# RWKV, HGRN and a weight stream on one TensorE: an order written by hand in place of the planner's

## Chip, cores and metric

One core of one Trainium2 chip runs the whole program. The metric is the device time of one execution in microseconds, the median of several runs. The engines are TensorE (PE, with its weight loads as PEld), VectorE (DVE), ScalarE (ACT), GpSimd (POOL) and SyncE (SP), which here only issues DMAs.

## The reference

One layer of a streaming encoder on 256 tokens of width 1024, float32. Three mixers run side by side on one combined projection of the normalised input, and a mixture of experts follows:

```
h = LN(x)
feats = h @ w_in          # SSD | RWKV-7 | HGRN2 | 3 gates
y_a = SSD(feats_a); y_b = RWKV7(feats_b); y_c = HGRN2(feats_c)
m = sum_i sigmoid(gate_i) * (y_i @ w_br_i)
h = LN(alpha*h + m @ w_out)
h = LN(alpha*h + MoE(h))  # 16 experts, top 1 group, top 2
```

RWKV is a recurrence over tokens (a delta rule: decay, rank-one correction, new key and value). HGRN is a gated linear recurrence. The kernel computes both in four chunks of 64 tokens: inside a chunk with matrices, from chunk to chunk with a state.

## The kernel before

**Weight streams.** Nearly all matrix work with weights from memory goes through `stream` (L331). SP loads four 128-row blocks of a 256-column slice (512 KB) into a `raw` buffer (L339, a ring of four). `split` (L180) makes two parts of each pair of blocks, `whi` by an ACT copy (L183) and `wlo` by a DVE subtraction (L184), each 128x512 and in a ring of four. Then PE makes six matmuls of 256 columns for each block, in a PSUM tile `st` of a ring of three: L366 to L368, or L358 to L360 where the tokens are the stationary side. Such six matmuls are called a pass here; `feat` (L371), one slice of 256 columns, is eight passes. Splits carry a priority far ahead of all else.

**The second half of the mixers** (`mixers`, L726) starts when the RWKV's preparations are done. In program order it holds these parts:

- `rwkv_solve` (L566): a triangular solve for a batch of two head pairs, 32 steps on DVE (L593, L595). Its operands come from DRAM, and its answer goes there (L599) and comes back in another layout (L605).
- `rwkv_solve_off` (L609): two DVE transposes of that answer (L618), 32 small matmuls (L623), two ACT copies, 32 more (L631) and two copies.
- `rwkv_b` (L637): the chain over four chunks, for two head pairs side by side. Each chunk has three steps: `w` (L654, and L658 from the state, then an ACT copy, L660), `u` (L662, ACT copies L663 and L665), and the state update (L670, then DVE at L674 or L676). Behind the chunks stand the outputs (L687, L691), their mean and variance, and the group norm (L694 to L708). `rwkv_out` (L710) transposes and finishes a pair (L715, L717, L722 to L724).
- `hgrn` (L838): three `feat` slices (q, v and gate), gates and exponentials on DVE, POOL and ACT, then four groups of PE work with ACT and DVE between them: L879 and L885, L893, L905 and L909, L920.
- `gates` (L780): eight more `feat` slices whose only successor is a tanh.

`rwkv_b`, `rwkv_out` and `hgrn` run four times (head pairs 0 and 1, 2 and 3, and so on), and `rwkv_solve_off` before the first and the third. The SSD mixer follows (`ssd_prep`, L989, with convolutions at L928 and L931), then the branches, the output projection and the experts.

**What sets the order.** The code is emitted in program order. A planner replays it against a timeline of its own and gives each engine its instructions in an order of priority and readiness; an instruction that is ready may so overtake others. On the chip each engine takes its queue in that order. `high_priority` moves a block ahead, `issue_after` holds one back. In the expert stage, `manual_schedule` already orders PE by hand: within its block the instructions of PE are issued as emitted.

The functions that the diff touches:

Of the kernel before, what the change touches and what calls it, by code (L numbers as in the profile page):

```python
# [7 lines left out]
F32 = mybir.dt.float32  # L8
# [5 lines left out]
OP = mybir.AluOpType  # L14
# [59 lines left out]
DNP = 60  # L74

# [64 lines left out]
class Kern:  # L140
# [190 lines left out]
    def stream(self, w, c0, ncol, xhi, xlo, ps, tokens):  # L331
# [5 lines left out]
        for kh in range(KT // KH):  # L337
# [11 lines left out]
            with self.tc.high_priority(offset=MMP):  # L349
                for kk in range(KH):  # L350
# [10 lines left out]
                    else:  # L361
                        for f in range(nf):
# [6 lines left out]
                                             stop=sp and f == nf - 1)  # L369

    def feat(self, c0, tokens=False, ncol=256, other=False):  # L371
        ps = self.pz.tile([128, 2, 256], F32, name="z") if other else self.pst.tile([128, 2, 256], F32, name="st")
        self.stream(self.A["w_in"], c0, ncol, self.hhi, self.hlo, ps, tokens)
        return ps
# [234 lines left out]
    def rwkv_solve_off(self, st):  # L609
# [23 lines left out]
        for h in range(2):  # L633
            q = slice(h * 64, h * 64 + 32)
            nc.scalar.activation(tt[q, :, 32:64], yps[q], AF.Copy)

    def rwkv_b(self, i0, st):  # L637
# [7 lines left out]
        zs = [self.zs[f] for f in range(2)]  # L645
        for c in range(4):
            for f in range(2):
                q = st["pairs"][i0 + f]
                sc, bkt, uv, ars, pe = (q[n] for n in ("sc", "bkt", "uv", "ars", "pe"))
                ch = banks[f][:, 0:192].rearrange("p (j n) -> p j n", j=3)  # L650
                z = zs[f]
# [11 lines left out]
                nc.scalar.activation(uv[hs[0], c, 0, :], ch[hs[0], 1, :], AF.Copy)  # L663
                if U1:
                    nc.scalar.activation(uv[hs[1], c, 1, :], ch[hs[1], 1, :], AF.Copy)  # L665
                else:
                    nc.vector.tensor_copy(uv[hs[1], c, 1, :], ch[hs[1], 1, :])
                if c < 3:
                    for h in range(2):
                        nc.tensor.matmul(ch[hs[h], 2, :], bkt[:, c, hs[h]], uv[:, c, h, :], start=True, stop=True,  # L670
                                         tile_position=(0, 64 * h))
                    for h in hs:
                        if c == 0:
                            nc.vector.tensor_copy(z[h, 0, h], ch[h, 2, :])  # L674
                        else:
                            nc.vector.scalar_tensor_tensor(z[h, c, h], z[h, c - 1, h], pe[h, c - 1:c], ch[h, 2, :],  # L676
                                                           op0=OP.mult, op1=OP.add)
# [30 lines left out]
        nc.vector.tensor_tensor(yc, yc, r[:, :, None].to_broadcast([128, 8, 64]), op=OP.mult)  # L708

# [16 lines left out]
    def mixers(self):  # L726
# [53 lines left out]
    def gates(self, ms):  # L780
        nc = self.nc
        for m in ms:
            ps = self.feat(COL_GATE + m * 256)
            nc.scalar.activation(self.gt[:, 2 * m:2 * m + 2, :], ps, AF.Tanh, scale=0.5)  # L784

# [51 lines left out]

    def hgrn(self, j):  # L838
# [4 lines left out]
        ps = self.feat(COL_Q + j * 256)  # L843
        q = a.new([128, 2, L], "q", 2)
# [899 lines left out]
```

## Time and profile before

| | us |
|---|---|
| median of 3 runs | 812.57 (811.85 to 814.41) |
| the profiled execution | 813.39 |
| its span, first to last instruction | 811.6 |
| PE busy | 777.7 (96%) |
| PE weight loads busy | 598.9 (74%) |
| DVE busy | 513.1 (63%) |
| ACT busy | 369.0 (45%) |
| mean granted clock of PE | 0.983 of full |

Matmuls are pipelined and their ends are modelled: in a view of the timeline, two matmuls that start 0.12 us apart each show 0.28 us. So the time that PE needs is read from start to start, and a PE that is busy in the table may still be off its best pace. The page divides the span into 40 slices, of 20.3 us each, and its digits are tenths. The second half of the mixers runs from about 168 to 424 us, the experts from about 575.

### The profile page before, as it was taken

What the parts mean: (1) busy time and instruction counts of PE and PEld (TensorE: products, weight loads), DVE (VectorE), ACT (ScalarE), POOL (GpSimd) and SP (SyncE); (2) the same over time, 40 slices, a digit from 0 to 9 for tenths busy, and PEclk for the clock granted to TensorE, in tenths of its full rate; (3) what the DMA queues carried; (4) which work ended last, traced back from release to release, by engine and by line L of the source; (5) the groups of instructions that cost most, each with busy time, mean ns of one, the idle gap of its engine ahead of it and who ended that gap; (6) DMA issues with size and microseconds to landing.
All of it is one profiled execution on the core that took longest, in us unless ns stands there. A gap on an engine that the chain in (4) does not pass through costs nothing. (4 is left out here: it accounts for less than half of the span.)

```text
span 811.6 us, 16395 instructions
## 1 busy us (share of the span) xinstructions
PE 777.7 (96%) x6306; PEld 598.9 (74%) x6306; DVE 513.1 (63%) x1166; ACT 369.0 (45%) x817; POOL 137.7 (17%) x211
## 2 busy tenths in 40 slices
PE   7999999999999999999998999999999999999991
PEld 5898899988997998998797999999444434443440
DVE  6897899999987555576589897785612211221146
ACT  4765555575446555645486764452512121211111
POOL 3364633631002002010012111000000000001201
PEclk9999999999999999999899999999999999999995
DMA  7544555493463463565188579995999999999961
GB/s 236 173 126 117 115 144 138 137 215 103 131 151 111 130 182 107 147 195 178 45 270 305 163 221 277 328 313 177 368 386 387 387 386 386 387 388 385 387 229 55
DMA packets 146493, 183.92 MB, mean 227 GB/s; under 512 B 25561, under 2 KB 94440, under 8 KB 146408
## 3 DMA queue, kind: packets, MB, share of 16 engines
q1 hardware_dynamic: 142888, 176.91, 66.5%
q0 software_dynamic: 1472, 3.21, 1.6%
q10 hardware_dynamic: 2048, 2.70, 1.1%
q8 instruction: 51, 0.84, 0.4%
q14 instruction: 34, 0.28, 0.1%
HBM read 180.13 MB, written 2.65 MB: 225 GB/s over the span
## 5 line engine op out<-in xcount | busy, mean ns | idle before, releaser
L184 DVE TENSOR_TENSOR wlo<-raw,whi 128x512 fp32r<-128x512 f32 x268 | 190.2, 720 | 75.2 <-ACT whi L183 64.1
L183 ACT ACTIVATE whi<-raw 128x512 fp32r<-128x512 f32 x268 | 165.0, 623 | 152.7 <-PE st L367 117.3
L366 PE MATMUL st<-hhi,whi 128*128 128x256 f32 (+1 forms) x744 | 209.6, 289 | 2.4 <-ACT arena L784 1.4
L368 PE MATMUL st<-hhi,wlo 128*128 128x256 f32 (+1 forms) x744 | 210.5, 292 | 0.8 <-DVE wlo L184 0.8
L367 PE MATMUL st<-hlo,whi 128*128 128x256 f32 (+1 forms) x744 | 207.8, 287 | 0.0
L368 PEld LDWEIGHTS st<-hhi,wlo 128*128 128x128 f32 (+1 forms) x744 | 139.4, 191 | 8.5 <-issue 3.9
L366 PEld LDWEIGHTS st<-hhi,whi 128*128 128x128 f32 (+1 forms) x744 | 140.0, 191 | 7.3 <-issue 2.4
L367 PEld LDWEIGHTS st<-hlo,whi 128*128 128x128 f32 (+1 forms) x744 | 139.7, 191 | 2.7 <-issue 1.4
L1455 PE MATMUL b<-arena,xg 128*64 128x512 f32 x288 | 78.8, 596 | 0.0
L367 PE MATMUL st<-ylo,whi 128*128 128x256 f32 x192 | 52.5, 284 | 1.9 <-DVE ylo L184 1.9
L366 PE MATMUL st<-yhi,whi 128*128 128x256 f32 x192 | 53.0, 284 | 0.3 <-ACT whi L183 0.2
L368 PE MATMUL st<-yhi,wlo 128*128 128x256 f32 x192 | 52.1, 283 | 0.0
L1455 PEld LDWEIGHTS b<-arena,xg 128*64 128x64 f32 x288 | 23.8, 137 | 38.0 <-issue 34.5
L1528 DVE SCALAR_TENSOR_TENSOR elo<-b,egs,ehi 128x512 fp32r<-128x512 f32 x15 | 11.2, 750 | 60.7 <-ACT ehi L1527 60.7
L1508 PE MATMUL b<-arena,ehT 128*64 128x512 f32 x144 | 43.0, 596 | 0.0
L367 PEld LDWEIGHTS st<-ylo,whi 128*128 128x128 f32 x192 | 35.5, 189 | 2.6 <-DVE ylo L184 2.3
L1497 ACT ACTIVATE ehT<-b 128x256 f32<-128x256 f32 x16 | 6.2, 390 | 68.1 <-PE b L1496 68.1
L366 PEld LDWEIGHTS st<-yhi,whi 128*128 128x128 f32 x192 | 35.7, 189 | 0.8 <-ACT whi L183 0.4
L1489 DVE SCALAR_TENSOR_TENSOR ehi<-ehi,b 128x256 f32<-128x256 f32 x16 | 6.0, 418 | 47.0 <-PE b L1455 47.0
L368 PEld LDWEIGHTS st<-yhi,wlo 128*128 128x128 f32 x192 | 35.4, 189 | 0.2 <-issue 0.2
L593 DVE TENSOR_TENSOR arena<-arena 128x1 f32<-128x1 f32 (+15 forms) x64 | 33.1, 517 | 1.0
L1370 POOL TENSOR_TENSOR arena<-arena 128x512 f32<-128x512 bf16 x4 | 4.5, 1156 | 171.6 <-PE b L1455 171.6
(453 smaller groups left out, 1432.2 us busy)
## 6 DMA issues: line engine op xcount, KB each, us to landing
raw<-in_w_in_dram SPq DMA_DIRECT2D x102, 512.0 KB, 3.7
arena<-in_exp_w_gate_dram SPq DMA_DIRECT2D x40, 512.0 KB, 10.7
arena<-in_exp_w_down_dram SPq DMA_DIRECT2D x34, 512.0 KB, 10.8
arena<-in_exp_w_up_dram SPq DMA_DIRECT2D x32, 512.0 KB, 10.8
xsl<-in_exp_w_up_dram SPq DMA_DIRECT2D x32, 512.0 KB, 10.8
xsl<-in_exp_w_down_dram SPq DMA_DIRECT2D x20, 512.0 KB, 10.8
xsr<-in_exp_w_gate_dram SPq DMA_DIRECT2D x16, 512.0 KB, 10.7
raw<-in_w_br_rwkv_dram SPq DMA_DIRECT2D x8, 512.0 KB, 4.2
```

What stands on the lines that cost most here:

```text
L183: nc.scalar.activation(hi, raw, AF.Copy)
L184: nc.vector.tensor_tensor(lo, raw, hi.bitcast(F32), op=OP.subtract)
L366: nc.tensor.matmul(o, hi[:, kq, fs], xhi[:, k, :], start=st and f == 0, stop=False)
L367: nc.tensor.matmul(o, hi[:, kq, fs], xlo[:, k, :], start=False, stop=False)
L368: nc.tensor.matmul(o, lo[:, kq, fs], xhi[:, k, :], start=False, stop=sp and f == nf - 1)
L593: nc.vector.tensor_tensor(po, tu[:, :n, :t + 1], eu[:, :t + 1, t][:, None, :].to_broadcast([128, n, t + 1]), op=OP.mult)
L1370: nc.gpsimd.tensor_tensor(o, x[1], x[2], op=OP.add)
L1455: nc.tensor.matmul(ps[hs[e]], xg[:, k, hs[e]], W[nm, e, k // 2][:, k % 2, :], start=k == 0, stop=k == KT - 1)
L1489: nc.vector.scalar_tensor_tensor(th[:, c], th[:, c], 0.5, q["pu"][:, c], op0=OP.mult, op1=OP.mult)
L1497: nc.scalar.activation(q["hT"][:, 2 * j:2 * j + 2], tp, AF.Copy)
L1508: nc.tensor.matmul(pd[hs[e], :], q["hT"][:, k, hs[e]], W["exp_w_down", e, (n, k // 2)][:, k % 2, :], start=k == 0, stop=k == 3)
L1528: nc.vector.scalar_tensor_tensor(lo, pd, q["gs"], hi.bitcast(F32), op0=OP.mult, op1=OP.subtract)
```

## The change

Four functions become generators that yield between their steps: `stream` (as `streaming`, one yield for each pass), `rwkv_solve_off` (two), `rwkv_b` (one for each step of a chunk) and `hgrn` (four). The three slices of `hgrn` become a generator of their own, `hgrn_in`; `rwkv_out` and one slice of `gates` get generators around them. In `rwkv_b` the two head pairs' parts of a step now stand together, where one pair's three steps stood ahead of the other's; nothing is computed otherwise. `interleave` runs them in turns inside a `manual_schedule` block for PE alone. A turn emits one step of the RWKV chain, one of the HGRN chain (a yield of n lets a chain rest for n turns) and FILL = 2 passes of the streams: `hgrn_in` in order, each as soon as the HGRN pair two before it is done, otherwise a gate slice, once the first RWKV pair is done. Passes that are left over come behind the chains. The second solve is emitted ahead of the first `rwkv_solve_off` instead of behind it.

```diff
-    def stream(self, w, c0, ncol, xhi, xlo, ps, tokens):
+    def stream(self, *a):
+        for _ in self.streaming(*a):
+            pass
+
+    def streaming(self, w, c0, ncol, xhi, xlo, ps, tokens):
...
+                    yield
...
+    def feating(self, c0, tokens=False):
+        ps = self.pst.tile([128, 2, 256], F32, name="st")
+        yield from self.streaming(self.A["w_in"], c0, 256, self.hhi, self.hlo, ps, tokens)
         return ps
...
         for c in range(4):
+            ws = []
             for f in range(2):
-                q = st["pairs"][i0 + f]
-                sc, bkt, uv, ars, pe = (q[n] for n in ("sc", "bkt", "uv", "ars", "pe"))
-                ch = banks[f][:, 0:192].rearrange("p (j n) -> p j n", j=3)
-                z = zs[f]
+                (sc, bkt, uv, ars, pe), ch, z = P[f], chs[f], zs[f]
...
+                ws.append(w)
+            yield 1
+            for f in range(2):
+                (sc, bkt, uv, ars, pe), ch, w = P[f], chs[f], ws[f]
                 for h in hs:
                     nc.tensor.matmul(ch[h, 1, :], tt[h, (i0 + f) * 4 + c, :], w[h], start=True, stop=True)
+                for h in range(2):
+                    nc.scalar.activation(uv[hs[h], c, h, :], ch[hs[h], 1, :], AF.Copy)
+            yield 1
+            if c == 3:
+                break
+            for f in range(2):
+                (sc, bkt, uv, ars, pe), ch, z = P[f], chs[f], zs[f]
+                for h in range(2):
+                    nc.tensor.matmul(ch[hs[h], 2, :], bkt[:, c, hs[h]], uv[:, c, h, :], start=True, stop=True,
+                                     tile_position=(0, 64 * h))
+                for h in hs:
...
+            yield 1
...
+    def rwkv_outs(self, i0, st):
+        for i in (i0, i0 + 1):
+            yield 1
+            self.rwkv_out(i, st)
...
         self.ssd_dt()
-        MARK('rwS')
-        self.rwkv_solve_off(s0)
-        MARK('rwS1')
         with self.tc.high_priority(offset=PSV):
             self.rwkv_solve(1, s1)
-        for j in range(4):
-            if j == 2:
-                MARK('rwS')
-                self.rwkv_solve_off(s1)
-            MARK('rwB%d' % j)
-            self.rwkv_b(2 * (j % 2), (s0, s1)[j // 2])
-            for i in (0, 1):
-                self.rwkv_out(2 * (j % 2) + i, (s0, s1)[j // 2])
-            MARK('hgrn%d' % j)
-            self.hgrn(j)
-        MARK('gates')
-        self.gates(range(NG - NZ - NY))
+        self.interleave(s0, s1)
...
+    def interleave(self, s0, s1):
+
+        self.hgin, done = [], dict(rw=0, hg=0)
+
+        def rwkv():
+            yield from self.rwkv_solve_off(s0)
+            for j in range(4):
+                st = (s0, s1)[j // 2]
+                if j == 2:
+                    yield from self.rwkv_solve_off(s1)
+                yield from self.rwkv_b(2 * (j % 2), st)
+                yield 4
+                yield from self.rwkv_outs(2 * (j % 2), st)
+                done["rw"] += 1
+                yield 1
+
+        def hgrn():
+            for j in range(4):
+                while len(self.hgin) <= j:
+                    yield 1
+                yield from self.hgrn(j)
+                done["hg"] += 1
+                yield 1
+
+
+        tiles = [(self.hgrn_in(j), lambda j=j: done["hg"] > j - 2) for j in range(4)]
+        gates = [(self.gating(m), lambda m=m: done["rw"] > 0) for m in range(NG - NZ - NY)]
+        queue, now = [tiles, gates], []
+
+        def fill():
+
+            while True:
+                if not now:
+                    for q in queue:
+                        if q and q[0][1]():
+                            now.append(q.pop(0)[0])
+                            break
+                    else:
+                        return False
+                try:
+                    next(now[0])
+                    return True
+                except StopIteration:
+                    now.clear()
+
+        chains = [[rwkv(), 0], [hgrn(), 0]]
+        with self.tc.manual_schedule(engines={mybir.EngineType.PE}):
+            while chains:
+                for c in list(chains):
+                    c[1] -= 1
+                    if c[1] <= 0:
+                        try:
+                            c[1] = next(c[0])
+                        except StopIteration:
+                            chains.remove(c)
+                for _ in range(FILL):
+                    fill()
+            while fill():
+                pass
...
+    def hgrn_in(self, j):
+
+        nc, a = self.nc, self.hga
+        ps = yield from self.feating(COL_Q + j * 256)
...
+        self.hgin.append((q, v, tg))
+
+    def hgrn(self, j):
+
+        nc = self.nc
+        a, mp = self.hga, self.pmm
+        hs = [slice(0, 64), slice(64, 128)]
+        q, v, tg = self.hgin[j]
...
```

## Rows read from the trace of the kernel before

**Rows 1.** Page, 40 slices: PE's busy time and granted clock in tenths

```profile
PE   7999999999999999999998999999999999999991
PEclk9999999999999999999899999999999999999995
```

**Rows 2.** Stretches: length, busy PE, PEld, DVE, ACT, POOL; clock, DMA, GB/s

```profile
220.00:240.00 20.00, 20.00 (x201) 18.99 (x200) 19.71 (x47) 9.87 (x21) 0.96 (x1) 1.00 0.55 144
...
380.00:400.00 20.00, 18.05 (x164) 13.77 (x163) 11.58 (x33) 8.58 (x32) 0.00 (x0) 0.83 0.18 54
```

**Rows 3.** PE's timeline, 387 to 400: start, duration, engine, line, [idle before, releaser]

```profile
387.70 0.34 PE L654 MATMUL ch<-arena 128*64 128x64 f32 x4
387.96 0.33 PE L658 MATMUL ch<-arena 64*64 64x64 f32 x4
...
390.46 0.81 PE L670 MATMUL ch<-arena 128*64 128x64 f32 x8 [0.43 <-ACT arena L665]
...
394.90 0.58 PE L366 MATMUL st<-hhi,whi 128*128 128x256 f32 x1
...
399.36 0.34 PE L654 MATMUL ch<-arena 128*64 128x64 f32 x4
```

**Rows 4.** PE's timeline, 222 to 226: a run of stream matmuls between two steps

```profile
222.44 0.39 PE L359 MATMUL st<-wlo,hhi 128*128 128x256 f32 x1
222.66 0.28 PE L367 MATMUL st<-hlo,whi 128*128 128x256 f32 x1
...
224.69 0.28 PE L360 MATMUL st<-whi,hlo 128*128 128x256 f32 x1
224.90 0.45 PE L662 MATMUL ch<-arena 64*64 64x64 f32 x8
225.27 0.39 PE L358 MATMUL st<-whi,hhi 128*128 128x256 f32 x1
```

**Rows 5.** PE's timeline, the two longest of its short waits

```profile
244.55 0.39 PE L359 MATMUL st<-wlo,hhi 128*128 128x256 f32 x1 [0.79 <-DVE wlo L184]
...
366.52 0.39 PE L366 MATMUL st<-hhi,whi 128*128 128x256 f32 x1 [1.09 <-ACT arena L784]
```

**Rows 6.** PE's timeline, 160 to 178

```profile
168.04 0.37 PE L358 MATMUL st<-whi,hhi 128*128 128x256 f32 x1
...
176.42 0.24 PE L623 MATMUL mm<-arena 32*32 32x32 f32 x2
```

**Rows 7.** SP's queue, 160 to 175: DMA issues

```profile
165.16 2.47 SPq L599 DMA_DIRECT2D td<-arena  x4
...
169.47 2.87 SPq L605 DMA_DIRECT2D arena<-td  x4
```

**Rows 8.** DVE's timeline, 175 to 176

```profile
175.91 0.70 DVE L618 STREAM_TRANSPOSE arena<-arena 32x512 f32<-32x512 f32 x1
```

**Rows 9.** All engines' timeline, 390 to 394: DVE and ACT of the chain

```profile
390.97 1.17 DVE L676 SCALAR_TENSOR_TENSOR arena<-arena,pe,ch 64x64 f32<-64x64 f32 x4
...
393.19 0.22 ACT L660 ACTIVATE arena<-ch 128x64 f32<-128x64 f32 x1 [0.68 <-PE ch L658]
```

**Rows 10.** DVE's groups of 168 to 235: count, busy us, mean ns, idle before

```profile
L593 DVE TENSOR_TENSOR arena<-arena 128x1 f32<-128x1 f32 (+31 forms) x32 | 16.6, 519 | 0.6
L595 DVE TENSOR_REDUCE arena<-arena 128x1 f32<-128x1 f32 (+31 forms) x32 | 10.9, 341 | 0.6
```

**Rows 11.** DVE's timeline, 290 to 302: the group norm of the second pair

```profile
292.74 0.42 DVE L694 TENSOR_REDUCE gmean<-ch 128x4 f32<-128x256 f32 x1 [0.48 <-PE ch L691]
...
301.17 0.68 DVE L708 TENSOR_TENSOR arena<-arena,gr_y 128x512 f32<-128x512 f32 x1
```

**Rows 12.** PE's groups of 168 to 427

```profile
L366 PE MATMUL st<-hhi,whi 128*128 128x256 f32 x400 | 112.9, 291 | 1.4 <-ACT arena L784 1.4
...
L358 PE MATMUL st<-whi,hhi 128*128 128x256 f32 x64 | 18.7, 292 | 0.0
```

**Rows 13.** Page, groups of the whole span: the streams' subtraction

```profile
L184 DVE TENSOR_TENSOR wlo<-raw,whi 128x512 fp32r<-128x512 f32 x268 | 190.2, 720 | 75.2 <-ACT whi L183 64.1
```

More of the change, by code (lines that the diff above doesn't have):

```diff
@@ L74 @@
 DNP = 60
+FILL = 2
 PARAMS = [("ln_in_g", 8), ("ln_in_b", 8), ("rwkv_mu", 26), ("rwkv_w0", 8), ("rwkv_a0", 8), ("rwkv_k_k", 8),
@@ L373, in feat @@
         self.stream(self.A["w_in"], c0, ncol, self.hhi, self.hlo, ps, tokens)
+        return ps
+    def feating(self, c0, tokens=False):
+        ps = self.pst.tile([128, 2, 256], F32, name="st")
+        yield from self.streaming(self.A["w_in"], c0, 256, self.hhi, self.hlo, ps, tokens)
         return ps
@@ L645, in rwkv_b @@
         zs = [self.zs[f] for f in range(2)]
+        P = [[st["pairs"][i0 + f][n] for n in ("sc", "bkt", "uv", "ars", "pe")] for f in range(2)]
+        chs = [banks[f][:, 0:192].rearrange("p (j n) -> p j n", j=3) for f in range(2)]
         for c in range(4):
+            ws = []
             for f in range(2):
-                q = st["pairs"][i0 + f]
-                sc, bkt, uv, ars, pe = (q[n] for n in ("sc", "bkt", "uv", "ars", "pe"))
-                ch = banks[f][:, 0:192].rearrange("p (j n) -> p j n", j=3)
-                z = zs[f]
+                (sc, bkt, uv, ars, pe), ch, z = P[f], chs[f], zs[f]
                 for h in range(2):
@@ L660, in rwkv_b @@
                 nc.scalar.activation(w, ch[:, 0, :], AF.Copy)
+                ws.append(w)
+            yield 1
+            for f in range(2):
+                (sc, bkt, uv, ars, pe), ch, w = P[f], chs[f], ws[f]
                 for h in hs:
                     nc.tensor.matmul(ch[h, 1, :], tt[h, (i0 + f) * 4 + c, :], w[h], start=True, stop=True)
[L663 to L677, printed above, removed]
+                for h in range(2):
[9 more added lines that the diff above has]
+                for h in hs:
+                    if c == 0:
+                        nc.vector.tensor_copy(z[h, 0, h], ch[h, 2, :])
+                    else:
+                        nc.vector.scalar_tensor_tensor(z[h, c, h], z[h, c - 1, h], pe[h, c - 1:c], ch[h, 2, :],
+                                                       op0=OP.mult, op1=OP.add)
+            yield 1
         mean = tp.tile([128, 8], F32, name="gmean")
@@ L784, in gates, with gating @@
             nc.scalar.activation(self.gt[:, 2 * m:2 * m + 2, :], ps, AF.Tanh, scale=0.5)
+    def gating(self, m):
+        ps = yield from self.feating(COL_GATE + m * 256)
+        self.nc.scalar.activation(self.gt[:, 2 * m:2 * m + 2, :], ps, AF.Tanh, scale=0.5)
+    def interleave(self, s0, s1):
[14 more added lines that the diff above has]
+                while len(self.hgin) <= j:
+                    yield 1
+                yield from self.hgrn(j)
+                done["hg"] += 1
+                yield 1
+        tiles = [(self.hgrn_in(j), lambda j=j: done["hg"] > j - 2) for j in range(4)]
[8 more added lines that the diff above has]
+                            break
+                    else:
+                        return False
[18 more added lines that the diff above has]
+                pass
     def hgrn_bounds(self):
@@ L836, in hgrn_start @@
         self.gyc, self.gy2 = self.rwa.new([128, 8, 64]), self.rwa.new([128, 8, 64])
+    def hgrn_in(self, j):
+        nc, a = self.nc, self.hga
+        ps = yield from self.feating(COL_Q + j * 256)
+        q = a.new([128, 2, L], "q", 2)
+        nc.scalar.activation(q, ps, AF.Tanh, scale=0.5)
+        nc.vector.scalar_tensor_tensor(q, q, 1.0, ps, op0=OP.add, op1=OP.mult)
+        ps = yield from self.feating(COL_I + j * 256, True)
+        v = a.new([128, 2, 256], "hv", 2)
+        nc.scalar.activation(v, ps, AF.Copy)
+        ps = yield from self.feating(COL_G + j * 256)
+        tg = a.new([128, 2, L], "tg", 2)
+        nc.scalar.activation(tg, ps, AF.Tanh, scale=0.5)
+        nc.gpsimd.tensor_scalar(tg, tg, self.hnw, self.hnw, op0=OP.mult, op1=OP.add)
+        self.hgin.append((q, v, tg))
     def hgrn(self, j):
```

15 lines of the change are left out of this document (4 added, 11 removed).

## The prediction, made before the change was run

> **What bounds the kernel now.** I read the page's slices first. TensorE (PE) is busy in nine tenths or more of all 40 slices but the first, the last and one at 8, and the granted clock is at its full 2.4 GHz in nearly all of them; one slice of the second half of the mixers shows 8 [rows 1]. So the time is PE's, and a change of PE's order can win only where PE waits, where its clock is halved, or where the switch between kinds of work costs issue time. Then the table by stretches: in the mixers PE is busy all the time with VectorE (DVE) close behind (19.71 of 20.00 us at 220 to 240), and one stretch, 380 to 400, has PE at 18.05, clock 0.83 and DMA at 54 GB/s [rows 2]. In the expert stage, the last 11 slices but one, PE has its nines throughout [rows 1]: it never waits there, so whatever the mixers gain or lose arrives at the end unchanged. Third, the order of PE's instructions, in which the whole argument lies.
>
> **What the change removes.** The planner's order left these holes in the stretch from 168 to 427 us. The largest is at the last RWKV pair: from 387.70 on no stream matmul is issued, the chain's steps wait for each other (0.43 us before L670, and others), and the clock falls; the next stream begins at 394.90, and its 21 matmuls up to 399.36 take 4.46 us, 0.21 each instead of 0.12 [rows 3, 4]. From 387.70 to 399.36, 11.7 us, PE does six small steps, some 3.6 us at full clock (0.37 us for eight matmuls [rows 4], 1.05 for a chunk's first step, four groups of 0.26), and the 21 stream matmuls, 2.5 us; with switches 6.3. Loss: 5.4 us. Four smaller holes in the same view, of 0.79, 1.09 (the two longest [rows 5]), 0.27 and 0.28 us, make it 7.8 us. The new order has work for this hole: counting turns, the RWKV chain has some 76, the four hgrn_in tiles and eight gates hold 12 x 8 + 8 x 8 = 160 passes, that is 80 turns of two, and the streams run out only as the chain ends. So I take the 7.8 us as gone (all of it is the upper bound; the 0.79 may return, because its cause, a DVE transpose that waits for a DMA, stays in the program).
>
> **What it does not remove.** A pass is six matmuls, 0.72 us. Each break of a stream by a chain step costs about 0.2 us: the last stream matmul to the step takes 0.21 instead of 0.12, and the first one behind it 0.22 [rows 4]. The planner breaks the streams 72 times from 176 to 424 us (runs in PE's timeline, of which rows 4 is one); the hand order breaks them about once a turn, 77 times, though both pairs' steps now stand together. I count zero, from -6 us (some twenty steps that are now cut in two are joined, 0.3 us each) to +1.
>
> **What it adds at the start.** This is the largest single term. In the region PE follows the order in which the code emits, and the first thing that the chains emit is rwkv_solve_off(s0): two DVE transposes and then the L623 matmuls. Before, PE is done with the SSD's dt matmuls at 168.0, and goes straight into stream passes of the first HGRN tile (the first at 168.04); L623 begins at 176.42 [rows 6]. That date isn't the planner's choice: the solve's answer is written to DRAM from 165.16 and read back from 169.47 [rows 7], and the second transpose that needs it starts at 175.91 and takes 0.70 [rows 8], so L623 can't start before 176.4. Every pass of the tile now stands behind L623. Earlier PE work there is none; later streams (SSD's) take the same rings of raw, whi and wlo buffers behind the tile's own, so they can't move up. PE idles from 168.0 to 176.4: 8.4 us. Splits for eight passes can be done meanwhile, but these are no PE time. The clock: after the thin stretch before 394.90 the 21 stream matmuls ran at 1.2 GHz and lost 1.9 us before it rose again [rows 3]. I take 2 after the new gap, which is longer and emptier (0 to 3.4, the second if the steps before them count too). The solve of the second batch is now emitted ahead of these transposes too, so on DVE it goes first when both are ready; its operations of the first steps are short, so I add nothing, at most 1 us.
>
> **What it adds turn by turn.** A turn is one RWKV step (0.37 us for eight matmuls [rows 4], 1.05 for the first step of a chunk), an HGRN step in 24 of the turns, and 12 x 0.12 = 1.44 us of streams. Between two steps of the RWKV chain PE has therefore some 1.6 us of cover where no HGRN step stands; the planner left 19 to 25 stream matmuls, 2.3 to 3.0 us. What must fit is best read where nothing covered it: the four state updates take 1.17 us from 390.97 and end 1.7 us after the first L670 at 390.46, of which 0.4 is the step itself, so 1.3; the copies of w and u are shorter (0.22 us each on ACT, two or four a step) [rows 3, 9]. All fit into 1.6 where ACT and DVE are free. But each turn also brings ACT a copy of 128x512 and DVE a subtraction of that size (0.72 us) [rows 13] for the streams, and these engines take their queues in order. One such piece in front turns 1.3 into 2.0, so the update waits 0.4 us in perhaps half of 12 cases, 2.4 us; the other steps have more room, 1 us together. In the first 24 turns DVE carries the second solve as well, 16.6 + 10.9 us of multiplies and sums [rows 10], emitted ahead of the chain and so preferred. DVE was busy 19.7 of 20 us there [rows 2] at the planner's slower pace; the hand order wants a chunk in three turns, some 7 us, of a DVE that is already full: I take 4 us. The group norm of a pair took 9.1 us from its last sum (292.74) to its result (301.17 + 0.68) [rows 11], on top of which PE's own outputs come; the change gives it five turns, 5 x 1.6 plus an HGRN step or two, 8 to 10 us, so 0.5 us for each of four pairs, 2 us. The two PSUM banks of a pair come free only after the output's copy, sum and product, a little over 2 us, against one turn: 0.3 us three times. Sum: 10 us, from 2 (everything hidden) to 26 (0.35 us in each of some 76 turns).
>
> **Behind the region.** Before, the mixers had swallowed 240 passes from 168 to 427 us, by 3 x (400 + 64) recorded stream matmuls and a few per cent that the trace lacks [rows 12]: 160 of the mixers and 80 of the SSD. Those 80 now come behind the chains, with the SSD's convolutions on DVE and less to cover them: 0 us, from -2 to +4. On SP's queue the raw loads keep their order, one of 512 KB for four passes; a pass needs no more than before. ACT and POOL get the same instructions.
>
> **Sum.** The profiled execution took 813.39 us, 1.8 of which lie around its span of 811.6. 813.4 + 8.4 + 2 - 7.8 + 10 = 826.0; it lies 0.8 above the median of 812.57, so 825.
>
> **The skill's rule on busy time.** In 220 to 240 us weight loads fill 18.99 of 20.00 us, in 380 to 400 only 13.77 [rows 2]. The Trainium skill (Perfetto Trace Analysis, Identifying the Most-Contended Engine) says that matmul busy time is a poor measure of the headroom and that the weight loads' busy share is a better one. By it the mixers outside the hole have about 5% left, and the hole a third; on the trace this agrees with the breaks of 0.2 us and the half clock, which the busy column does not show. It would allow a better order to win where the busy column allows nothing, which is the first rival.
>
> **Rivals.** *Faster:* the joined steps save up to 6 us of breaks, the chains are covered, and the hole is gone: 813.4 + 10.4 - 7.8 - 6 + 2 = 812, and if the start gap is shorter by half (the read-back lands earlier than its transposes say), 807. For it speaks that steps of both pairs stand together; against it the DMA dates. It decides at stalls under 2 us and a gap under 6. Chance 0.11 for under 810. *No difference:* gap and hole cancel, nothing else: 811 to 815, chance 0.12. *Covered:* gap and clock, but no turn waits: 813.4 + 2.6 + 1 - 0.8 = 816, chance 0.18. *Every turn waits:* ACT's and DVE's queues put one piece more before each step: 813.4 + 2.6 + 26 - 0.8 = 841, chance 0.14; the solve's preference on DVE speaks for it, the idle DVE after 240 us against it. *Forecast:* 818 to 833, chance 0.45.
>
> **How the numbers follow.** A measurement of this kernel tells about 0.3%, 2.4 us, from no change. Faster 0.11, same 0.12, slower 0.18 + 0.14 + 0.45 = 0.77. The range leaves out the faster case and the top half of the last: 811 to 840.
>
> **What would show it.** Right: PE idle for 7 to 9 us just before L623's first matmul, ended by DVE's transpose, and a slice with clock under 1.0 behind it; no thin stretch at the last pair; PE idle of 0.2 to 1 us before the state-fed step while the second solve runs, and before the output transposes. Wrong: stream matmuls of the first tile before L623; waits before most chain steps; or the SSD beginning on a stalled DVE.

## The result: slower by 4 per cent, and where the time went

The changed kernel takes 844.52 us (median of 4 runs, 842.36 to 847.2); the kernel before takes 812.21 beside it. The ratio is 1.0397, 95% interval 1.0352 to 1.0441. The profiled execution spans 844.5 us, against 811.6. The forecast of 825 had the sign; the loss was 32 us instead of 12.6.

The page's slices of the changed kernel, PE's busy time and granted clock in tenths (before: [rows 1]):

```profile
PE   7999999679779999699999989999999999999991
...
PEclk9999999969879999699999999999999999999996
```

Three dents have come where there was one: about 160, 230 and 345 us (a slice is 21.1 us here). In each the clock falls as well. The table by stretches, with the columns of [rows 2]:

```profile
160.00:180.00 20.00, 6.84 (x83) 5.70 (x84) 15.53 (x38) 10.07 (x18) 6.71 (x9) 0.62 0.57 123
...
220.00:240.00 20.00, 9.81 (x62) 7.81 (x64) 14.10 (x32) 5.46 (x12) 4.08 (x4) 0.75 0.27 55
340.00:360.00 20.00, 13.88 (x86) 10.15 (x86) 9.57 (x31) 5.12 (x19) 1.46 (x2) 0.66 0.35 98
380.00:400.00 20.00, 18.52 (x181) 17.52 (x180) 11.77 (x29) 13.01 (x30) 3.54 (x4) 1.00 0.82 267
```

From 220 to 240 PE was busy for 20.00 of 20 us before; now for 9.81. The thin stretch of before, 380 to 400, has gone from a clock of 0.83 to 1.00, as forecast. What PE waited for, from 160 to 450 (line that waited, releaser: us in all, times, longest):

```profile
PE ch L741 <- DVE arena L727: 16.3, 4, 7.0
PE mm L1061 <- DVE dtx L1056: 8.1, 1, 8.1
PE mm L634 <- DVE arena L629: 5.2, 2, 4.8
PE ch L667 <- DVE arena L748: 4.7, 1, 4.7
...
```

L741 are the RWKV's output transposes, which want the group norm's last product (L727). L1061 are the SSD's dt sums (L977 of before), L634 is the first correction step (L623 of before), L667 a pair's first step, which wants the PSUM bank of the pair before it. PE's timeline has the dates of the longest:

```profile
167.97 0.58 PE L1061 MATMUL mm<-dtx,tri 128*128 128x16 f32 x2 [8.08 <-DVE dtx L1056]
...
175.54 0.28 PE L634 MATMUL mm<-arena 32*32 32x32 f32 x2 [4.83 <-DVE arena L629]
...
225.51 0.47 PE L741 MATMUL ch<-ident,arena 128*128 128x128 f32 x1 [6.32 <-DVE arena L727]
...
237.60 0.48 PE L667 MATMUL ch<-arena 128*64 128x64 f32 x4 [4.68 <-DVE arena L748]
...
346.01 0.47 PE L741 MATMUL ch<-ident,arena 128*128 128x128 f32 x1 [6.97 <-DVE arena L727]
```

To see the rest of the loss I added up PE's timeline by kind of neighbour: the distance from each matmul's start to the next one's, with idle times over 0.05 us taken out, from the 766th to the 2323rd recorded stream matmul (from just ahead of the chains into the SSD, the same count of streams in each kernel). A stream matmul is here one that reads the normalised input (`hhi`, `hlo`); "step" is any other; in brackets how often a stream is broken. All in us:

| kernel | in all | stream to stream | stream to step | step to stream | step to step | idle |
|---|---|---|---|---|---|---|
| before | 295.9 | 187.7 | 15.2 (76) | 10.9 | 73.2 | 8.9 |
| changed | 329.3 | 189.4 | 15.4 (77) | 10.3 | 77.1 | 37.2 |
| changed, planner's order | 358.8 | 191.7 | 35.8 (145) | 21.7 | 85.0 | 24.6 |
| before, joined steps, solve ahead | 294.9 | 187.1 | 15.2 (76) | 10.9 | 73.4 | 8.4 |
| hand order, split solve | 295.6 | 188.0 | 15.3 (77) | 9.7 | 68.7 | 13.9 |
| hand order, longer rests | 286.0 | 187.4 | 15.0 (78) | 9.7 | 66.3 | 7.6 |

The second row against the first: 33.4 us, of which 28.3 are idle PE. Ahead of the stretch the two kernels are within 0.4 us of each other, and behind it the changed kernel takes 358.7 us and the kernel before 359.6, so the whole loss is in it. The other 5.1 us are what is left of two larger changes. Matmuls are farther apart where the granted clock is at the lower of its two levels, 1.2 GHz (the first and the last of the five dt matmuls start 2.13 us apart from 167.97 on, 1.30 before): 258 distances lie there, and together they are 13.3 us longer than the means of the same pairs of instructions at 2.4 GHz in that trace; in the kernel before there are 43, with 2.9 us. So half clock costs some 10 us more, and by difference some 5 us come back: full-clock steps are denser in the hand order. The other rows are those of experiments below.

### The profile page after: what moved, and what is told of

Read it like the earlier page. It is cut to its first block, busy times and chain, and to the rows that moved or that the text cites. A ratio compares the mean times of both kernels' runs of the same rounds, so it can differ in the third digit from the quotient of the medians.

```text
span 844.5 us, 16405 instructions
## 1 busy us (share of the span) xinstructions
PE 778.3 (92%) x6306; PEld 600.5 (71%) x6306; DVE 515.5 (61%) x1166; ACT 370.7 (44%) x817; POOL 137.5 (16%) x211
## 5 line engine op out<-in xcount | busy, mean ns | idle before, releaser
L185 DVE TENSOR_TENSOR wlo<-raw,whi 128x512 fp32r<-128x512 f32 x268 | 188.1, 709 | 75.3 <-ACT whi L184 70.3
L371 PE MATMUL st<-hhi,whi 128*128 128x256 f32 (+1 forms) x744 | 215.0, 295 | 0.9 <-ACT whi L184 0.9
L373 PEld LDWEIGHTS st<-hhi,wlo 128*128 128x128 f32 (+1 forms) x744 | 141.4, 192 | 6.3 <-DVE wlo L185 2.4
L372 PEld LDWEIGHTS st<-hlo,whi 128*128 128x128 f32 (+1 forms) x744 | 141.6, 193 | 1.8 <-issue 1.1
L604 DVE TENSOR_TENSOR arena<-arena 128x1 f32<-128x1 f32 (+15 forms) x64 | 32.5, 508 | 1.3
## 6 DMA issues: line engine op xcount, KB each, us to landing
arena<-in_exp_w_gate_dram SPq DMA_DIRECT2D x40, 512.0 KB, 10.7
xsr<-in_exp_w_gate_dram SPq DMA_DIRECT2D x16, 512.0 KB, 10.7
x<-in_exp_w_gate_dram SPq DMA_DIRECT2D x8, 512.0 KB, 10.7
```

The costliest lines, as they stand in the source:

```text
L185: nc.vector.tensor_tensor(lo, raw, hi.bitcast(F32), op=OP.subtract)
L371: nc.tensor.matmul(o, hi[:, kq, fs], xhi[:, k, :], start=st and f == 0, stop=False)
L372: nc.tensor.matmul(o, hi[:, kq, fs], xlo[:, k, :], start=False, stop=False)
L373: nc.tensor.matmul(o, lo[:, kq, fs], xhi[:, k, :], start=False, stop=sp and f == nf - 1)
L604: nc.vector.tensor_tensor(po, tu[:, :n, :t + 1], eu[:, :t + 1, t][:, None, :].to_broadcast([128, n, t + 1]), op=OP.mult)
```

## Experiments

Theory A: every long wait has its own late result, and the order written out by hand keeps streams behind it that the planner would have put under it. Rivals: the turns are too short for the steps; the hand order only passes a wait on; or joined steps, more breaks or the moved solve cost the time. Each time is a median; ratios are to the kernel before, measured beside it.

**The start: sixteen passes ahead of the chains.**

```
         with self.tc.manual_schedule(engines={mybir.EngineType.PE}):
+            for _ in range(16):
+                fill()
             while chains:
```

> 16 passes of the first HGRN tile are emitted ahead of the chains, so PE has streams while the first solve's answer travels through DRAM. Theory A (fixed order meets late inputs: the waits before L1061 and L634, 13.3 us, and the half clock behind them): both waits shrink below 2 us and the kernel comes to about 832 us, since the chains' last eight turns lose their streams. Rival B (turns too short for the chain's round trip): the gap only moves, 842 us or more. Rival C (80 stream passes pushed behind the region make the SSD stage slow): no change, 844 us.

830.34 us, ratio 1.0198 (1.0156 to 1.0241): 14.2 less. PE's waits in the run (lines are one further on):

```profile
PE mm L1007 <- ACT hr L1003: 9.6, 2, 8.5
PE ch L742 <- DVE arena L728: 6.4, 2, 5.5
PE mm L635 <- DVE arena L605: 2.6, 1, 2.6
...
```

Streams may stand ahead of the solve's answer, and then most of the gap is covered: of 13.3 us 4.6 are left (2.6 and 1.1 before L635, 0.9 before the dt sums). The wait near 230 did not go. It now stands before the HGRN's output transposes, whose norm waits on the same VectorE.

**The second solve's preference on VectorE taken away** (`PSV = -600` for 0).

> One constant: the second batch's solve gets a priority 600 instructions later, so that it no longer goes ahead of the chain on DVE. Theory A (the output transposes L741 wait for a group norm that stands behind foreign DVE work; for the first pair that is the solve): the waits of 6.32 and 4.68 us at the first pair's output go below 2 us each, with the half clock behind them about 10 us, 834 us. Rival B (turns too short): under 3 us. Rival C: no change. If the solve then comes too late for the third pair, a new wait stands before the second L634.

849.55 us, ratio 1.043 (1.0383 to 1.0477): a miss, no gain on the changed kernel. The wait before L741 near 225 is 4.11 us instead of 6.32, the one before L667 5.66 instead of 4.68, and those before L634 at the start grow from 5.2 to 8.2. VectorE's timeline of this run shows why the edit does little:

```profile
212.44 0.76 DVE L713 TENSOR_REDUCE gmean<-ch 128x4 f32<-128x256 f32 x2
213.11 1.01 DVE L604 TENSOR_TENSOR arena<-arena 128x450 f32<-128x450 f32 x1
214.04 0.17 DVE L716 TENSOR_SCALAR gmean<-gmean 128x8 f32<-128x8 f32 x1
214.16 0.62 DVE L606 TENSOR_REDUCE arena<-arena 128x15 f32<-128x450 f32 x1
...
```

Each operation of the norm needs the one before it. The planner still puts pieces of the solve (L604, L606) between them, of 0.6 to 1.1 us, three of each instead of five: the norm takes 12.9 us instead of 15.1, but starts 2.1 us later. One explanation is that a piece of the solve is ready whenever the norm's next operation is not, so that a lower preference does not keep it out; a later run tests that. This one does not say whether the solve is the cause.

**The residual held back.** The two products of the output projection's residual (L1240, L1241) may issue only behind the last RWKV product.

```
+            with self.tc.issue_after(self.mixed.ins):
                 nc.vector.scalar_tensor_tensor(h[:, t, :], h[:, t, :], mv[:, t, 0:1], g, ...)
                 nc.vector.scalar_tensor_tensor(h[:, t, :], h[:, t, :], r[:, t:t + 1], b, ...)
```

In the changed kernel VectorE's timeline has them inside the third pair's group norm, and its queue stands for a DMA that the first of them wants:

```profile
328.73 0.76 DVE L721 TENSOR_TENSOR arena<-ch,gmean 128x256 f32<-128x256 f32 x2
333.18 2.48 DVE L1240 SCALAR_TENSOR_TENSOR arena<-arena,li_mv 128x1024 f32<-128x1024 f32 x2 [3.69 <-DMA arena<-in_ln_in_g_dram]
...
337.02 0.67 DVE L724 TENSOR_REDUCE gvar<-arena 128x8 f32<-128x512 f32 x1
...
339.81 2.47 DVE L1241 SCALAR_TENSOR_TENSOR arena<-arena,ln_r_y 128x1024 f32<-128x1024 f32 x2
```

> The residual's two DVE operations for each token half (L1240, L1241), which wait for a DMA and which the planner put into the third pair's group norm, are held behind the last output product of the RWKV. Theory A: the wait of 6.97 us before the third pair's L741 falls to the 1.5 us of the second and fourth pairs, and the half clock behind it goes: about 9 us, 835 us. Rival B and rival C: 844 us.

836.67 us, ratio 1.0281 (1.0231 to 1.0332): 7.9 less. The wait of 6.97 us is gone, and the norm of that pair takes 10.7 us instead of 18.6; the others stay:

```profile
PE ch L741 <- DVE arena L727: 9.3, 3, 6.3
...
```

**The changed emission, with the planner's order on PE** (all else as changed).

```
-        with self.tc.manual_schedule(engines={mybir.EngineType.PE}):
+        with ExitStack():
```

> The same emission (turns, joined steps, solve ahead of the chains) without the block that fixes PE's order: the planner orders PE again. Theory A (the fixed order is the cost): back to 812 to 820 us. Rival C (the emission itself, and the SSD's streams behind it, are the cost): above 830 us.

879.01 us, ratio 1.0802 (1.0754 to 1.085). Theory A of this run is refuted: that PE's order is fixed is not by itself the cost, since without it the same emission takes 35 us more. It is what rival C allowed (above 830), but not for the SSD's streams: behind the stretch of the table it takes 359.7 us, as the kernel before does. The planner, given steps and passes turn by turn, cuts a step into pieces of two matmuls with one or two stream matmuls between them:

```profile
331.07 0.24 PE L634 MATMUL mm<-arena 32*32 32x32 f32 x2
331.25 0.38 PE L371 MATMUL st<-hhi,whi 128*128 128x256 f32 x1
331.56 0.24 PE L634 MATMUL mm<-arena 32*32 32x32 f32 x2
331.73 0.50 PE L372 MATMUL st<-hlo,whi 128*128 128x256 f32 x2
```

In the table above streams are broken 145 times instead of 76, and the two columns of breaks hold 31.4 us more (35.8 + 21.7 - 15.2 - 10.9). But each of the 69 more breaks also takes a distance of 0.13 us out of a stream and one of 0.06 out of a step, 13 us, so that they cost some 18 us, 0.27 each; the prediction read 0.2 from [rows 4]. Idle PE is 15.7 us more, and half clock, counted as above, 18.0 us instead of 2.9 (part of it falls on the breaks).

**The two cures together.**

> The sixteen passes ahead of the chains and the held residual together, to see whether the two gains add. Theory A (each of the long waits has a cause of its own: the start gap, the residual in the third pair's group norm): 844.5 - 14.2 - 7.8 = 822.5, 820 to 825, with the wait of 8.5 us near 230 still there. Rival B (TensorE's fixed order only passes a wait on to the next late result): 828 to 831, with waits of 5 us or more also behind 330.

825.2 us, ratio 1.0159 (1.0127 to 1.019). They add nearly (822.5 expected, 825 at most). One long wait is left, 8.64 us near 230, and only one further of over 2.3.

**The second solve only behind the first pair's norm**, on top of both:

```
+                if j == 0:
+                    with self.tc.issue_after(self.normed.ins):
+                        self.rwkv_solve(1, s1)
                 yield 4
```

> As the run with both edits, and the second solve is emitted and released only behind the first pair's group norm, so that its 26.7 us of multiplies and sums cannot stand between the norm's steps. Theory A (the second solve on VectorE makes the first pair's results late): the wait of 8.5 us near 230 goes and with it some 2 us at half clock, 811 to 813; the second solve's answer is needed about turn 39 and arrives in time. Rival C (the streams' subtractions and the few turns alone make it late): the wait stays above 5 us, 819 to 823. Rival D (the answer now comes too late for the third pair): a new wait before the second batch's first correction step, 5 us or more, 815 to 825.

832.03 us, ratio 1.024 (1.0199 to 1.0282): slower than everything that was expected. Both halves of the answer are in the waits: the one near 230 shrinks to 1.94 us, the first pair's norm takes 9.0 us instead of 12.6. But the solve now fills VectorE from 240 to 280 (19.57 and 19.66 us of each 20), and the second pair is late, with a norm of 17.0 us instead of 11.8:

```profile
PE ch L742 <- DVE arena L728: 9.6, 2, 7.2
PE mm L1008 <- ACT hr L1004: 7.4, 2, 5.5
...
```

So the solve makes the norm late beside which it runs, the first or, moved, the second: where its pieces stand among a norm's steps is what decides.

**Longer rests instead**, on top of both, behind a pair's steps and behind the HGRN's norm:

```
-                yield 4
+                yield 7 if j in (0, 2) else 4
...
-        yield 4
+        yield 8
```

> As the run with both edits, with longer rests: seven turns instead of four behind the first and the third pair's last step, eight instead of four behind the HGRN's norm; solve as in the changed kernel. Theory A (the results are late by a fixed amount of VectorE work, and turns can cover it): the wait of 8.5 us near 230 shrinks to under 3, but the streams run out at turn 72 of 83, so that the last pair's last steps stand bare, 3 to 5 us: 816 to 819. Rival B (a wait only moves): 820 to 825.

820.84 us, ratio 1.01 (1.0076 to 1.0124): within rival B's range, not theory A's. The waits of the later pairs go from 0.84 and 2.48 to 1.70 and none, but 8.64 us before the first HGRN output stay as they were. This is a fault of the edit: the third tile's streams are let in only behind the first tile's output, so that these added turns had no pass in them.

**What the parts cost under the planner.** The kernel before, with the residual held:

> The kernel before with the held residual alone. Theory A (the planner puts streams under a late group norm, so the residual costs TensorE nothing there): no difference, ratio 0.997 to 1.003. Rival (the residual delays the last pair there too, and the thin stretch of 380 to 400 comes from it): 3 to 6 us faster, 807 to 810.

815.21 us, ratio 1.0025 (1.0006 to 1.0045): no gain. In the kernel before, the third norm took 17.4 us too, with the residual in it, but the planner had streams under it:

```profile
353.41 0.42 DVE L694 TENSOR_REDUCE gmean<-ch 128x4 f32<-128x256 f32 x1 [0.17 <-PE ch L691]
...
358.56 2.48 DVE L1156 SCALAR_TENSOR_TENSOR arena<-arena,li_mv 128x1024 f32<-128x1024 f32 x2 [0.53 <-DMA arena<-in_ln_in_g_dram]
...
370.12 0.68 DVE L708 TENSOR_TENSOR arena<-arena,gr_y 128x512 f32<-128x512 f32 x1
```

Held back, it leaves a norm of 9.9 us, and the time is no shorter. Next, the joined steps alone, the loop of `rwkv_b` as the change's diff has it:

> The kernel before, in the planner's order, with only the RWKV's steps rewritten as the change does it: both heads' groups of a pair stand together, step by step. Theory A (the joined steps save nothing that can be measured, and are not what made the changed emission 66 us slower under the planner): 810 to 816. Rival (some twenty joined steps save 0.3 us of breaks each): 806 to 809. Rival (a joined step waits for the later of its two halves): 820 or more.

813.53 us, ratio 1.0 (0.9986 to 1.0014). And with the second solve emitted ahead as well:

```
-        self.rwkv_solve_off(s0)
         with self.tc.high_priority(offset=PSV):
             self.rwkv_solve(1, s1)
+        self.rwkv_solve_off(s0)
```

> The kernel before under the planner, with the joined steps and with the second solve emitted ahead of the first solve's answer, as the change has it; chains and tiles are emitted in the old sequence. Theory A (these two parts of the change cost nothing; under the planner it is the emission turn by turn that cost 66 us, and with the hand order it is waiting): 811 to 816. Rival (the moved solve delays the first chain on VectorE): 818 or more.

814.81 us, ratio 0.9993 (0.9973 to 1.0013). These two runs say less than they seem to: in their traces PE, VectorE, ScalarE and GpSimd have the same sequence of operations, tiles and shapes as in the kernel before, from first to last. The planner came to the same order either way, so neither edit was tried. That joined steps and the breaks of the hand order cost nothing to speak of is shown by the hand orders below, which keep both and come to 814.94 and 802.3 us.

**Covering what is late.** The third tile's streams are let in at the first tile's output products, the dt sums stand in the hand order behind four passes, sixteen passes follow, rests are longer, and an RWKV chunk's first step gets one pass instead of two. (`hgops` counts the tiles whose output products are emitted.)

```
-... lambda j=j: done["hg"] > j - 2 ...
+... lambda j=j: self.hgops > j - 2 ...
...
-                yield 4
+                yield (9, 4, 6, 4)[j]
...
-        yield 4
+        yield 4 if j else 8
```

> The hand order with its late results covered: the residual held; four passes ahead of the SSD's dt sums (their matmuls moved into the hand order) and sixteen behind them; nine turns of rest instead of four behind the first pair, six behind the third, eight behind the first HGRN norm; the third tile's streams allowed once the first tile's output products stand, so that the longer rests have passes in them; one pass instead of two in the turns of an RWKV chunk's first step, which pays for the longer rests. Theory A (the whole loss is TensorE standing before results that are late by a known amount, and the clock behind these stands): 820.8 of the run with longer rests, less 8.6 at 230 us, less 3.4 at the start, less 2 to 3 of half clock: 806 to 812, equal to the kernel before or better. Rival B (a fixed order only passes a wait on): 817 to 822. Rival E (turns of one pass are too short for the step): waits of 0.3 us or more before most second steps of a chunk, 812 to 817.

824.85 us, ratio 1.0133 (1.0116 to 1.0151): worse than the run with plain longer rests, and above even rival B's range. The first norm now takes 20.7 us; PE comes to its outputs 11 us later than it came to the first late result before (232.5 instead of 221.1), and still waits:

```profile
PE ch L742 <- DVE arena L728: 6.0, 1, 6.0
...
```

More turns alone are no cover here: on VectorE seven pairs of the solve's pieces and ten subtractions now stand between the norm's operations. Next, two passes in every turn again, and the solve cut in two:

```
-            self.rwkv_solve(1, s1)
+            self.solve_rest = self.rwkv_solve(1, s1, 24)   # steps 0 to 23
...
+                if j == 0:
+                    with self.tc.issue_after(self.normed.ins):
+                        self.solve_rest()                   # steps 24 to 31
```

> As the run with covered results (held residual, dt sums after four passes, sixteen passes behind them, third tile's streams allowed at the first tile's output products), but with two passes in every turn and rests of 5, 4, 6, 4 turns behind the pairs and 6 behind the first HGRN norm; and the last 8 of the second solve's 32 steps, 13 us of VectorE's work, released only behind the first pair's group norm. Theory F (between two of the norm's some 20 dependent operations VectorE takes one or two long pieces that stand ready, whatever their preference; only work that isn't released yet stays out): first pair's norm in 9 to 12 us instead of 14 to 21, wait there under 2 us, 810 to 814. Rival G (VectorE is simply full from 140 to 240, so the same work comes later and another step waits for it): a wait of 4 us or more between 230 and 300, 817 to 824.

814.94 us, ratio 0.9997 (0.9981 to 1.0014): theory F in its mechanism, its time missed by 0.9 us. The hand order is as fast as the planner's. Passes and rests changed too, so how much of the 9.9 us is the split's is not shown; what it does to the norm is. VectorE's timeline of the first norm has no solve between its steps any more, only subtractions (L185) and two products of the HGRN, and it takes 10.6 us:

```profile
215.83 0.76 DVE L722 TENSOR_REDUCE gmean<-ch 128x4 f32<-128x256 f32 x2
216.62 0.17 DVE L725 TENSOR_SCALAR gmean<-gmean 128x8 f32<-128x8 f32 x1
216.82 0.76 DVE L730 TENSOR_TENSOR arena<-ch,gmean 128x256 f32<-128x256 f32 x2
218.25 0.69 DVE L185 TENSOR_TENSOR wlo<-raw,whi 128x512 fp32r<-128x512 f32 x1 [0.68 <-ACT whi L184]
219.04 0.69 DVE L733 TENSOR_REDUCE gvar<-arena 128x8 f32<-128x512 f32 x1
...
225.71 0.69 DVE L736 TENSOR_TENSOR arena<-arena,gr_y 128x512 f32<-128x512 f32 x1
```

Two waits of over 3 us were left, before the dt sums and before the second HGRN output. Two orders cover them, one just these (below), one with longer rests everywhere:

```
-            for _ in range(4): ...      # passes ahead of the dt sums
+            for _ in range(9): ...
-            for _ in range(16): ...     # passes behind them
+            for _ in range(8): ...
```

> As the run with the split second solve, whose profile still shows TensorE waiting 3.3 us before the SSD's dt sums and 3.4 us before the second HGRN tile's output transposes, and 1.3 us behind the first pair's outputs: nine passes instead of four ahead of the dt sums and eight instead of sixteen behind them; six turns of rest instead of four behind the second HGRN norm; two turns instead of one behind the first pair's outputs. Theory A (a covered hand order also gets back the short waits that the planner's order has, the term of 7.8 us of the sum): 814.9 - 3.3 - 3.4 - 1 = 807, 805 to 810, ratio 0.988 to 0.994. Rival B (VectorE is the bound of 160 to 260 us, so a covered wait comes back at the next late result): 812 to 816, ratio 0.997 to 1.002.

> As the run before it, with still longer rests everywhere: 6, 5, 6, 4 turns behind the pairs' last steps, 3, 2, 2, 1 behind their outputs, and 6, 7, 6, 4 behind the HGRN's norms. Theory A: what is covered stays covered, the streams end six turns earlier against the chains, and the SSD's first streams fill the last pair's turns: within 2 us of the run before it. Rival H (passes taken early are missing at the end): 4 us or more slower than the run before it.

816.1 and 801.93 us, neither as its theory A said; but in both the second tile's q overwrites the first's before that was read, so neither computes the reference. With the buffer put right:

> The run with nine and eight passes at the start and the few longer rests once more, with the small buffer of the dt sums taken ahead of the first tile's (in the run before it the second tile's q came into the first tile's buffer while that was still to be read). The reuse had also set waits, so: Theory A: 805 to 812, ratio 0.988 to 0.997. Rival B (a covered wait comes back): 812 to 817.

> The run with longer rests everywhere once more, with the same buffer put right. Theory A: 799 to 804, ratio 0.983 to 0.988, no wait of TensorE above 2 us between 180 and 360: the covered hand order gets back the 7.8 us of the planner's short waits and a little more. Rival B: 810 or more.

816.89 us, ratio 1.0032 (1.001 to 1.0055), and 802.3 us, ratio 0.9864 (0.9836 to 0.9891). The first is a miss, as rival B said: the two waits are gone, and PE idles as long as in the split-solve run (14.0 us against 13.9), in many short waits, and breaks its streams 85 times instead of 77. The second is as theory A said, and faster than the kernel before by 11 us (813.76 beside it). All its waits of PE from 160 to 430:

```profile
PE st L373 <- DVE wlo L185: 2.8, 3, 1.5
PE st L371 <- ACT whi L184: 2.7, 2, 1.5
PE ch L676 <- DVE arena L703: 1.2, 2, 0.9
PE st L364 <- DVE wlo L185: 0.4, 1, 0.4
```

and the stretch that lost most, where VectorE is as full as in [rows 2]:

```profile
220.00:240.00 20.00, 20.00 (x190) 17.63 (x189) 19.50 (x41) 9.94 (x26) 3.10 (x4) 1.00 0.43 132
```

The last row of the table tells where the 9.9 us of that row's gain come from: 1.3 are idle time, 6.9 lie between steps (about 1 of it is half clock of the kernel before). The last run also holds the residual, splits the solve and moves the dt sums; under the planner only the first of these was tried, so it isn't shown that a hand order alone gives the 11 us.

## Why the prediction was wrong in size

**The sum.** Forecast were 8.4 + 2 - 7.8 + 10 = 12.6 us. In the table the change costs 28.3 us of idle PE and some 10 of half clock, and gets some 5 back in denser steps. Three terms were mis-sized: the start gap, the half clock and, above all, the wait for the group norms.

**The start gap, 8.4 us, measured 13.3.** The mechanism was right: PE stands because everything emitted later stands behind L634. The step that failed is "PE idles from 168.0 to 176.4". I took the dt sums' date from before and took for granted that PE is busy until then. Ahead of them the planner had streams of the first tile as well, as the kernel before shows:

```profile
165.21 0.28 PE L366 MATMUL st<-hhi,whi 128*128 128x256 f32 x1
166.50 0.40 PE L977 MATMUL mm<-dtx,tri 128*128 128x16 f32 x2 [1.01 <-DVE dtx L972]
```

These streams are behind L634 now too: PE stands from 159.9, for 8.08 us before L1061, then for 4.83 and 0.36 before L634. The 16 passes ahead gave 14.2 us back.

**The half clock, 2 us, measured some 10** (13.3 against 2.9 before). The mean granted clock was 0.62 in 160 to 180, which the term was for, but also 0.75 and 0.83 in 220 to 260 and 0.66 in 340 to 360, where PE stood 6.32, 4.68 and 6.97 us. The waits that the sum lacked brought their own half clock with them.

**Chain steps: no waits where I put them, 16.3 us where I put 2.** "The state update waits 0.4 us in perhaps half of 12 cases, 2.4" and 1 for the rest: the trace has no wait over 0.11 us before any step of a chunk but the first one of the second pair. "The group norm of a pair took 9.1 us ... so 0.5 us for each of four pairs": this is the mis-sized term, with 6.32, 1.50, 6.97 and 1.48 us. I had read one norm of four [rows 11]. From first sum to result the four took 14.3, 10.0, 17.4 and 12.2 us in the kernel before, which the trace would have told. By the prediction's own count five turns cover 8 to 10. "I take 4 us" for the second solve on VectorE was put before the chain's steps; it came before the outputs. PSUM banks: 0.9 forecast, 4.7 measured, because the output's copy, sum and product stood behind HGRN work: the copy (L746) starts on ScalarE only at 235.01, behind an HGRN operation that waited 3.23 us for GpSimd, and the product (L748) ended the wait at 237.6.

In the changed kernel's first norm, on VectorE's timeline, one sees the pattern that the sum lacked:

```profile
210.36 0.76 DVE L713 TENSOR_REDUCE gmean<-ch 128x4 f32<-128x256 f32 x2
211.03 0.87 DVE L604 TENSOR_TENSOR arena<-arena 128x392 f32<-128x392 f32 x1
211.83 0.16 DVE L716 TENSOR_SCALAR gmean<-gmean 128x8 f32<-128x8 f32 x1
211.94 0.56 DVE L606 TENSOR_REDUCE arena<-arena 128x14 f32<-128x392 f32 x1
212.42 0.75 DVE L721 TENSOR_TENSOR arena<-ch,gmean 128x256 f32<-128x256 f32 x2
213.08 1.00 DVE L604 TENSOR_TENSOR arena<-arena 128x435 f32<-128x435 f32 x1
213.99 0.69 DVE L185 TENSOR_TENSOR wlo<-raw,whi 128x512 fp32r<-128x512 f32 x1
...
224.77 0.69 DVE L727 TENSOR_TENSOR arena<-arena,gr_y 128x512 f32<-128x512 f32 x1
```

Among the 18 operations of the norm, from its first sum to its result, stand 17 long pieces of other work, ten of them the solve's: 15.1 us for what took 9.0 with the solve out of the way. It is hardly longer than the 14.3 us of the kernel before; there the planner had streams under it.

**The holes of before, 7.8 us.** Gone at 380 to 400, as said, but other stands took their place. Even the last run has 7.6 us of idle PE, against 8.9 before, and 1.5 us of half clock, against 2.9.

**Switches: zero, from -6 to +1.** The breaks cost the same (77 for 76, 25.7 us in the two columns for 26.1). What the hand orders save lies between steps: 4.5 us in the split-solve run and 6.9 in the last. In the changed kernel half clock hides it: 20.8 of its 77.1 us between steps ran at 1.2 GHz. This is near the -6 that I set down for joined RWKV steps, but by luck: no breaks were saved, and from one RWKV matmul to the next it is only 29.5 us before, 28.0 and 27.3 there. The rest lies in the HGRN's groups and between groups of different kinds: the steps of both chains stand in 149 unbroken groups of one kind before and in 114 in both of these runs. That whole steps are the reason fits this; no run tests it alone.

**"Every turn waits", 841 us,** came nearest in time and is refuted as a mechanism: no turn was too short for its step. The Trainium skill's rule that the headroom is better read from the weight loads' busy share (Perfetto Trace Analysis, Identifying the Most-Contended Engine) left room of about 5% outside the hole, by the one stretch that the prediction read; the best order found here gains 1.4% of the whole, within that room.

## What to carry to other kernels

An order written out by hand turns each late result into a stand of that engine with all that is queued behind it; so before it is fixed, list for each step the slowest of all the dates at which its input came in the trace, not one of them, and put that much independent work in front. Where a chain of short operations shares an engine with long ones, a lower preference was little help (12.9 us for 15.1); what kept the long ones out was to hold them until the chain had ended. Held whole, they made the next chain late instead (832 us); held in part, with passes and rests fitted to it, they did not (814.94). Compare orders with a table of idle time, breaks and pitch: here they lie 77 us apart (879 and 802) at nearly the same instructions.

## What was not expected of the hardware

A break of a stream takes 0.20 us into the step and 0.14 back in 76 breaks, 0.25 and 0.15 in 145 (15.2 / 76, 10.9 / 76, 35.8 / 145, 21.7 / 145), half clock included. So one break costs little more when breaks are frequent. Of the changed kernel's 33.4 us some 10 are half clock, behind waits that add up to 7 to 13 us at each of three places in an otherwise full stretch: around the stands of 6.32 and 4.68 us, 12 apart, the mean granted clock was 0.75 in 220 to 240 and 0.83 in 240 to 260. In the last run, with waits of at most 1.5 us, it is 1.00 from 160 to 380.

Open is why the order with only two waits covered gained nothing while the one with longer rests gained 14 us; the table of its waits shows that they came back in pieces, not which rest was the one that counted.
